# Pairing the experts of a mixture layer to the last one, and moving a run-time branch behind the last expert's products

## The chip, the cores and the metric

The kernel runs on one core of a Trainium2 chip. Its engines are named as in the profile: PE is TensorE (matrix products) and PEld its weight loads, DVE is VectorE, ACT is ScalarE, POOL is GpSimd, and SP is SyncE, which here issues nearly all DMAs. The metric is the device time of one execution in microseconds (us), taken as the median of several runs. A profiled execution has a span (first to last instruction) and its own time, which is slightly longer.

## The reference

Two layers, each a mixer (three kinds of attention) followed by a hierarchical mixture of experts over 256 tokens with 1024 channels. The change is in the mixture:

```python
def hier_moe(h, w_gr, b_gr, w_er, b_er, w1, w3, w2):
    ...   # top-1 group of 4, top-2 of its 8 experts: 512 assignments to 32 experts
    def expert_ffn(args):
        xb, e = args
        return (jax.nn.silu(xb @ w1[e]) * (xb @ w3[e])) @ w2[e]
    ...   # rows gathered in blocks of one expert, results weighted and added back per token
x = x + gt2 * hier_moe(h, ...)
```

w1 and w3 are 1024 x 384 and w2 is 384 x 1024 for each of the 32 experts, all float32.

## The kernel before

The order of the work on each engine is written out by hand: every engine executes its instructions in the order in which the Python code emits them, and waits on semaphores where data or a buffer is missing. A matrix product is emitted through the helper `mm` (line 102), so nearly all products carry that line and are told apart by the tiles that they write: `A` (first products of an expert), `O` (second products), `y` (the sums per token), `ga` (the gather), `uT` (transposes), `PTe` (one-hot transposes).

`moe(l)` gives each expert a block of 64 slots. One-hot matrices (`onehot`, line 1557) gather the tokens of four experts at a time: `gather_piece(q, i)` does 8 products into a bank `ga`, which ACT scales out into `xT` (line 1582); four pieces make one group of four experts. Then a loop runs over the experts e = 0 to 31. Its parts are:

- `ffn1(e)`: 16 products with w1 and w3 into `A` (recorded as two groups of 16 instructions, one for each of the two weight pieces of 1536 KB), on even e also `places` (line 1594), then silu on ACT (line 1632) and gate and product on DVE (line 1633) into `u`. Two experts of a pair share one `u`, in its two halves of 64 partitions, where `paired(e)` holds.
- `tr_pair(e)` (lines 1646 and 1648): three transposes of a whole pair's `u` and one ACT copy to `uT`; or `tr(e)` (lines 1658 and 1661): the same for one expert.
- `ffn2(e)`: 6 products (12 instructions) with w2, the third weight piece, into `O`, then two DVE products with the layer's gate (line 1693). After the odd expert of a pair, ACT and DVE split the result into two parts (lines 1699 and 1700).
- `combine(p, js)`: products that add the parts of pair p into the four `y` banks, one half of the channels for each j.

The loop is staggered up to e = 23: it emits ffn1(e), a half of an older combine, tr_pair on odd e, two gather pieces on odd e up to 27, and then ffn2(e-1), so that the second products of an expert stand behind the first ones of the next. From e = 24 (`ATONCE`) on each expert is done at once: ffn1(e), combine, gather, tr(e), ffn2(e). The last pair is combined behind the loop, straight from float32.

`overflow` (from line 1789) handles experts with more than 64 tokens. Every engine loads a count from SBUF into a register (line 1794) and branches over a loop (line 1798) that is entered only where the count is above zero; with these inputs it isn't entered. Behind the branch each engine sets semaphores, since waits behind it count on what the loop would have signalled. Before the change it stands ahead of ffn1(30).

The weights come as one stream of DMAs in a fixed order (`pump`, line 85): 94 pieces of 1536 KB for the experts' loop of a layer and 6 smaller ones that are loaded ahead. A piece is issued when fewer than `ring` pieces are held (6, and 8 from e = 26), so when PE is through with an older one. Behind layer 0's experts the stream goes on with layer 1's mixer: a piece of its input projection, then pieces of the modulation (`ada`).

Behind the loop of layer 0 the next mixer's first steps are emitted (`next(self.mixing)`), then combine(15); in layer 1 combine(15) is followed by the copies and the DMAs of the output.

Of the kernel before, what the change touches and what calls it, by code (L numbers as in the profile page):

```python
# [17 lines left out]
NE, SLOTS = 32, 64  # L18
# [19 lines left out]
class Kern:  # L38
# [1373 lines left out]
    def moe(self, l):  # L1412
# [15 lines left out]
        y = [[self.bank('y') for _ in range(2)] for _ in range(2)]  # L1428
# [4 lines left out]
        xhi, xlo = ([self.alloc('w', [128, 1024], F32R, 'xp') for _ in range(2)] for _ in range(2))  # L1433
# [37 lines left out]
        Mf, G, R = (RT[:, i * 64:i * 64 + 64].rearrange("p (t n) -> p t n", t=2) for i in range(3))  # L1471
# [21 lines left out]
        gt = self.gate_halves(l)  # L1493
# [34 lines left out]
        def blocks():  # L1528

            cnt, nb, cum, tt = (RT[:, 192 + 32 * i:224 + 32 * i] for i in range(4))  # L1530
            V.tensor_scalar(nb, cnt, float(SLOTS), None, op0=ALU.is_gt)
            for k in (2, 3):
                V.tensor_scalar(tt, cnt, float(SLOTS * k), None, op0=ALU.is_gt)
                V.tensor_add(nb, nb, tt)
            cur, other = cum, tt
            V.tensor_copy(cur, nb)
            for s in (1, 2, 4, 8, 16):
                V.tensor_copy(other[:, :s], cur[:, :s])
                V.tensor_add(other[:, s:32], cur[:, s:32], cur[:, :32 - s])
                cur, other = other, cur  # L1540
            nov = self.cp.tile([128, 4], I32, name=f"nov_{l}", tag='nov')
            V.tensor_copy(nov[:, 0:1], cur[:, 31:32])
            start = RT[:, 320:352]
            V.tensor_sub(start, cur, nb)
            return nov, nb, start
        a2, s2 = ab[:, 0:8], ab[:, 8:16]
# [13 lines left out]
        def onehot_b(q):  # L1560
            V.tensor_copy(PO[q][1], PO[q][0])

        def gather_piece(q, i):

            P, _ = PO[q]
            if i == 0:
                for h in range(2):
                    XT[q, h] = self.alloc('w', [128, 8, 128], F32, 'xT')
            ps = self.bank('ga')
            for k in range(2):  # L1570
                kt = 2 * i + k
                n = 0
                for t in range(2):
                    for part in (xhi, xlo):
                        self.mm(ps[:, k * 256:k * 256 + 256], part[t][:, kt * 128:kt * 128 + 128],
                                P[:, t].rearrange("p e s -> p (e s)"), n == 0, n == 3)
                        n += 1
            for k in range(2):
                kt = 2 * i + k
                for h in range(2):  # L1580
                    dst, src = XT[q, h][:, kt], ps[:, k * 256 + h * 128:k * 256 + h * 128 + 128]
                    nc.scalar.activation(dst, src, AF.Identity, scale=a2[:, kt:kt + 1], bias=s2[:, kt:kt + 1])  # L1582
            self.free(ps)
# [52 lines left out]
            E[e] = u  # L1636

        def paired(e):
            return e < ATONCE

        def tr_pair(e):

            u = E[e]
            p = self.bank('uT')
            for f in range(3):
                nc.tensor.transpose(p[:, f * 128:f * 128 + 128], u[:, f * 128:f * 128 + 128], self.ident)
            uT = self.alloc('s', [128, 3, 128], F32, 'uT')
            nc.scalar.activation(uT, p[:, :384].rearrange("p (f s) -> p f s", f=3), AF.Copy)
            self.free(p, u)
            E[e - 1], E[e] = uT[:, :, 0:64], uT[:, :, 64:128]  # L1650
            UT[e] = uT

        def tr(e):
            u = E[e]
            b = 64 * (e % 2)
            p = self.bank('uT')
            for f in range(3):
                nc.tensor.transpose(p[:, f * 64:f * 64 + 64], u[b:b + 64, f * 128:f * 128 + 128],  # L1658
                                    self.ident[b:b + 64, b:b + 64])
            uT = self.alloc('s', [128, 3, 64], F32, 'uT')  # L1660
            nc.scalar.activation(uT, p[:, :192].rearrange("p (f s) -> p f s", f=3), AF.Copy)  # L1661
            self.free(p, u)
            E[e] = UT[e] = uT
# [3 lines left out]
        def ffn2(e):  # L1667
            uT = E[e]
            key = ('e', l, e, 2)
            if key in self.beside(l):  # L1670
                w = [self.pieces[key + (f,)] for f in range(3)]
            else:
                u = self.take(key)
                w = [u[:, 1024 * f:1024 * f + 1024] for f in range(3)]
            n = 256 if e == NE - 1 else 512
            o = {c: self.bank('O') for c in range(0, 512, n)}
            for c in range(0, 512, n):
                for f in range(3):
                    for h in range(2):
                        self.mm(o[c][64 * h:64 * h + 64, :n], uT[:, f], w[f][:, 512 * h + c:512 * h + c + n], f == 0, f == 2)  # L1680
            if key in self.beside(l):
                self.free(*w)
            else:
                self.done(key)
            if e in UT:
                self.free(UT.pop(e))
            if e % 2 == 0:
                O[e // 2] = self.alloc('w', [128, 1024], F32, 'O')
            b = 64 * (e % 2)
            for c in range(0, 512, n):  # L1690
                for h in range(2):
                    p = slice(64 * h, 64 * h + 64)
                    V.tensor_mul(O[e // 2][b:b + 64, 512 * h + c:512 * h + c + n], o[c][p, :n], gt[p, c:c + n])  # L1693
            self.free(*o.values())
            if e % 2 and e < NE - 1:

                whole = O[e // 2]
                hi, lo = O[e // 2] = [self.alloc('w', [128, 1024], F32R, 'Op') for _ in range(2)]
                nc.scalar.activation(hi, whole, AF.Copy)  # L1699
                V.tensor_sub(lo, whole, hi)  # L1700
                self.free(whole)

        def combine(p, js=(0, 1)):
            last = p == 15
            parts = [O[p]] if last else O[p]
            for j in js:
                n = 256 if last else 512
                for c in range(0, 512, n):
                    for t in range(2):
                        to = PT[p][:, t * 128:t * 128 + 128]  # L1710
                        for part in parts:
                            self.mm(y[t][j][:, c:c + n], to.bitcast(F32) if last else to, part[:, 512 * j + c:512 * j + c + n],
                                    False, last and c + n == 512)
            if js[-1]:
                self.free(*parts)
                if p % 2:
                    self.free(PTQ[p // 2])


        ATONCE = 24  # L1720

        def rest_of_first():
            gather_piece(0, 2)
            gather_piece(0, 3)
            onehot(1)
            onehot_b(1)

        onehot(0)
        gather_piece(0, 0)
        gather_piece(0, 1)  # L1730
        G3 = gates_and_blocks()
        onehot_b(0)
        nov, nb, start = blocks()
        for e in range(NE):
            if e == NE - 6:
                self.ring = 8
            if e == ATONCE:
                ffn2(e - 1)
            if e == NE - 2:
                self.overflow(l, xhi, xlo, R, G, nb, start, nov, gt, a2, s2, y)  # L1740
            if e:
                ffn1(e)
            else:
                ffn1(0, rest_of_first)
            if 4 <= e < ATONCE + 2:
                combine(e // 2 - 2, (e % 2,))
            if e < ATONCE and e % 2:
                tr_pair(e)
            if e // 4 < 7 and (e % 2 if e > 3 else e > 1):
                for i in range(2):  # L1750
                    gather_piece(e // 4 + 1, (e % 4 - 1 if e > 3 else 2 * e - 4) + i)
                if e % 4 == 3 and e // 4 < 6:
                    onehot(e // 4 + 2)
                    onehot_b(e // 4 + 2)
            if e >= ATONCE:
                combine(e // 2 - 1, (e % 2,))
                tr(e)
                ffn2(e)
                continue
            if e:  # L1760
                ffn2(e - 1)
        self.free(*xhi, *xlo)
        if self.mixing:
            nc.scalar.preload_act_table_set(EXP_LN)
# [211 lines left out]
```

## Time and profile before

| | |
|---|---|
| median of 3 runs | 1390.2 us (1389.4 to 1391.21) |
| profiled execution, its own time | 1390.37 us |
| span of that execution | 1388.6 us |
| PE busy | 1329.2 us (96%) |
| PEld, DVE, ACT, POOL busy | 63%, 48%, 39%, 10% of the span |
| DMA | 437.95 MB, mean 315 GB/s |
| mean granted TensorE clock | 0.989 |

The experts' loop of layer 0 runs from about 369 to 715 us of the span, that of layer 1 from about 1038 to 1384 us. The granted clock is a share of 2.4 GHz; the other level is 1.2 GHz. A busy PE includes products that run at the slower level.

### The profile page before, as it was taken

How to read it: one execution, taken by the hardware profiler on the slowest of the kernel's cores; microseconds unless marked ns; L12 is line 12 of the kernel's file. 1: busy time of each engine (PE TensorE's matmuls, PEld its weight loads, DVE VectorE, ACT ScalarE, POOL GpSimd, SP SyncE). 2: the span in 40 equal slices, each digit the busy share in tenths (PEclk: the TensorE clock that was granted, in tenths of full speed). 3: DMA queues.
4: the chain of work that ended last, by engine and by line, in shares of the span. 5: the costliest groups of instructions: out<-in, count | busy, mean ns of one | idle time of the engine just before them, and what ended most of it. 6: DMA issues, size and time to landing. Idle time of an engine off the chain costs nothing. (4 is left out here: it accounts for less than half of the span.)

```text
span 1388.6 us, 19465 instructions
## 1 busy us (share of the span) xinstructions
PE 1329.2 (96%) x7666; PEld 869.3 (63%) x7666; DVE 668.2 (48%) x1417; ACT 538.4 (39%) x1140; POOL 135.2 (10%) x138
## 2 busy tenths in 40 slices
PE   5999999999899999999899999999999999999997
PEld 3788787887544444444358897888764444444443
DVE  5587564676623223332256775556762233323222
ACT  4554554574322222221155565447532222222211
POOL 0002064300100000000000202641010000000000
PEclk9999999999999999999999999999989999999999
DMA  9965457369589999999993626525858999999993
GB/s 373 374 246 222 184 204 289 129 246 360 222 345 425 425 425 424 425 426 425 420 421 151 227 91 232 191 94 202 358 214 318 404 425 425 425 424 427 424 424 147
DMA packets 45215, 437.95 MB, mean 315 GB/s; under 512 B 5080, under 2 KB 5608, under 8 KB 11328
## 3 DMA queue, kind: packets, MB, share of 16 engines
q1 hardware_dynamic: 44832, 435.78, 77.2%
q8 instruction: 62, 1.02, 0.3%
q0 software_dynamic: 288, 0.89, 0.2%
q14 instruction: 33, 0.27, 0.1%
HBM read 435.59 MB, written 1.05 MB: 314 GB/s over the span
## 5 line engine op out<-in xcount | busy, mean ns | idle before, releaser
L102 PE MATMUL in<-h,hH 128*128 128x384 f32 (+1 forms) x576 | 206.1, 358 | 3.7 <-ACT hH L1345 2.5
L1693 DVE TENSOR_TENSOR O<-O,gth 64x512 f32<-64x512 f32 (+1 forms) x132 | 88.8, 673 | 243.2 <-PE O L102 242.2
L102 PE MATMUL in<-h,hL 128*128 128x384 f32 (+1 forms) x576 | 195.3, 339 | 0.1
L102 PE MATMUL in<-l,hH 128*128 128x384 f32 (+1 forms) x576 | 194.5, 338 | 0.0
L1632 ACT ACTIVATE u<-A 64x384 f32<-64x384 f32 x64 | 31.1, 487 | 300.9 <-PE A L102 300.9
L102 PEld LDWEIGHTS in<-h,hH 128*128 128x128 f32 x576 | 109.0, 189 | 29.3 <-issue 17.1
L102 PEld LDWEIGHTS in<-h,hL 128*128 128x128 f32 x576 | 108.8, 189 | 1.4 <-DVE hL L1346 1.4
L102 PEld LDWEIGHTS in<-l,hH 128*128 128x128 f32 x576 | 109.2, 190 | 0.5
L1582 ACT ACTIVATE xT<-ga,modab 128x128 f32<-128x128 f32 x256 | 93.0, 468 | 20.6 <-PE ga L102 20.6
L1699 ACT ACTIVATE Op<-O 128x1024 fp32r<-128x1024 f32 x30 | 31.7, 1057 | 138.6 <-DVE O L1693 138.6
L1633 DVE SCALAR_TENSOR_TENSOR u<-A,m,u 64x384 f32<-64x384 f32 x64 | 39.4, 616 | 89.5 <-ACT u L1632 86.1
L102 PE MATMUL ga<-Poh,xp 128*128 128x256 f32 x512 | 71.4, 294 | 0.0
L102 PE MATMUL y<-Op,PTp 128*128 128x512 f32 x240 | 70.1, 415 | 0.0
L102 PEld LDWEIGHTS ga<-Poh,xp 128*128 128x128 f32 x512 | 65.8, 198 | 5.4 <-issue 4.0
L1602 DVE CAST PTp<-PTe 128x256 fp32r<-128x256 bf16 x32 | 13.6, 425 | 115.3 <-PE PTe L102 115.3
L803 POOL TENSOR_TENSOR rot<-TB,rope 128x256 f32<-128x256 f32 x8 | 11.7, 1487 | 488.6 <-ACT UC L873 429.3
L947 ACT ACTIVATE P<-P,m 128x256 f32<-128x256 f32 (+1 forms) x48 | 27.6, 576 | 79.2 <-DVE m L1005 37.1
L102 PEld LDWEIGHTS y<-Op,PTp 128*128 128x128 f32 x240 | 40.6, 188 | 21.0 <-issue 15.5
L1700 DVE TENSOR_TENSOR Op<-O,Op 128x1024 fp32r<-128x1024 f32 x30 | 36.8, 1225 | 33.8 <-ACT Op L1699 29.2
L1033 POOL TENSOR_SCALAR bias<-dist 128x128 f32<-128x128 f32 (+1 forms) x48 | 36.5, 761 | 5.2 <-PE oT L102 1.3
L1030 POOL TENSOR_SCALAR qz<-UC,gq 128x384 f32<-128x384 f32 x16 | 22.2, 1387 | 142.9 <-PE oT L102 72.7
L955 DVE TENSOR_SCALAR P<-P,m 128x256 f32<-128x256 f32 (+1 forms) x80 | 29.9, 407 | 1.8
(848 smaller groups left out, 2451.5 us busy)
## 6 DMA issues: line engine op xcount, KB each, us to landing
piece<-in_w_e SPq DMA_DIRECT2D x12, 512.0 KB, 6.8
w('ada', 0, 0, 0)_4_90<-in_w_ada SPq DMA_DIRECT2D x1, 1536.0 KB, 9.6
w('ada', 0, 0, 1)_5_92<-in_w_ada SPq DMA_DIRECT2D x1, 1536.0 KB
w('in', 0, 0)_9_104<-in_w_in SPq DMA_DIRECT2D x2, 768.0 KB, 16.5
w('in', 0, 1)_10_108<-in_w_in SPq DMA_DIRECT2D x2, 768.0 KB, 16.3
w('in', 0, 2)_11_110<-in_w_in SPq DMA_DIRECT2D x2, 768.0 KB, 12.2
w('ada', 0, 0, 3)_18_196<-in_w_ada SPq DMA_DIRECT2D x1, 1536.0 KB
w('ada', 0, 0, 4)_35_252<-in_w_ada SPq DMA_DIRECT2D x1, 1536.0 KB
```

The costliest lines, as they stand in the source:

```text
L102: self.nc.tensor.matmul(out, lhsT, rhs, start=start, stop=stop)
L947: nc.scalar.activation(dst, src, AF.Exp, bias=mx_neg[:, i:i + 1], scale=1.0, accum_out=sm[:, i:i + 1])
L955: nc.vector.tensor_scalar(dst, dst, r[:, i:i + 1], None, op0=ALU.mult)
L1030: nc.gpsimd.tensor_scalar(qz, M['qd'][:, pr::2, t * 128:t * 128 + 128], self.gq[:, l, 1 + hh:2 + hh], None, op0=ALU.mult)
L1033: nc.gpsimd.tensor_scalar(bias[:, lo:hi], self.dist[:, t, 256 + lo:256 + hi], -DIL_SLOPE[g][h], None, op0=ALU.mult)
L1582: nc.scalar.activation(dst, src, AF.Identity, scale=a2[:, kt:kt + 1], bias=s2[:, kt:kt + 1])
L1602: V.tensor_copy(PT[p], pv)
L1632: nc.scalar.activation(u[b:b + 64], A[c:c + 64, :384], AF.Silu)
L1633: V.scalar_tensor_tensor(u[b:b + 64], A[b:b + 64, :384], GC[e // 2][b:b + 64, e % 2:e % 2 + 1], u[b:b + 64], op0=ALU.mult, op1=ALU.mult)
L1693: V.tensor_mul(O[e // 2][b:b + 64, 512 * h + c:512 * h + c + n], o[c][p, :n], gt[p, c:c + n])
L1699: nc.scalar.activation(hi, whole, AF.Copy)
L1700: V.tensor_sub(lo, whole, hi)
```

## The change

The loop is staggered to the end: each expert's second products stand behind the next one's first products, ffn2(31) stands behind the loop, and behind it combine(14), the overflow branch, and combine(15). All experts but the first two are paired. The first two are transposed one by one, expert e-1 behind ffn1(e). In the turn of e = 3 the transposes of the pair are put between the products of the gather's first piece and that piece's ACT copies. The number of products is the same; the transposes of e = 24 to 31 become 4 pairs of them, those of e = 0 and 1 two single ones.

```diff
-        def gather_piece(q, i):
+        def gather_piece(q, i, between=None):
...
+            if between:
+                between()
             for k in range(2):
                 kt = 2 * i + k
                 for h in range(2):
...
         def paired(e):
-            return e < ATONCE
+            return e > 1
...
-        ATONCE = 24
...
         for e in range(NE):
             if e == NE - 6:
                 self.ring = 8
-            if e == ATONCE:
-                ffn2(e - 1)
-            if e == NE - 2:
-                self.overflow(l, xhi, xlo, R, G, nb, start, nov, gt, a2, s2, y)
             if e:
                 ffn1(e)
             else:
                 ffn1(0, rest_of_first)
-            if 4 <= e < ATONCE + 2:
+            if e >= 4:
                 combine(e // 2 - 2, (e % 2,))
-            if e < ATONCE and e % 2:
+            if 0 < e < 3:
+                tr(e - 1)
+            elif e % 2 and e > 3:
                 tr_pair(e)
             if e // 4 < 7 and (e % 2 if e > 3 else e > 1):
                 for i in range(2):
-                    gather_piece(e // 4 + 1, (e % 4 - 1 if e > 3 else 2 * e - 4) + i)
+                    gather_piece(e // 4 + 1, (e % 4 - 1 if e > 3 else 2 * e - 4) + i,
+                                 (lambda: tr_pair(3)) if e == 3 and i == 0 else None)
                 if e % 4 == 3 and e // 4 < 6:
                     onehot(e // 4 + 2)
                     onehot_b(e // 4 + 2)
-            if e >= ATONCE:
-                combine(e // 2 - 1, (e % 2,))
-                tr(e)
-                ffn2(e)
-                continue
             if e:
                 ffn2(e - 1)
+        ffn2(NE - 1)
+        combine(14)
+        self.overflow(l, xhi, xlo, R, G, nb, start, nov, gt, a2, s2, y)
         self.free(*xhi, *xlo)
```

## Rows read from the trace of the kernel before

**Rows 1.** Windows: length, each engine's busy time (instructions), clock, DMA share, GB/s.

```profile
1287.26:1359.99 72.73, 65.46 (x373) 30.52 (x369) 19.94 (x32) 14.72 (x32) 0.00 (x0) 1.00 1.01 422
```

**Rows 2.** Timeline of PE, staggered experts of layer 1: start, length, instruction, [idle before].

```profile
1225.01 2.75 PE L102 MATMUL A<-'e', 1, 18, 0)_2041_9981,xT 128*64 128x384 f32 x16
...
1234.18 2.75 PE L102 MATMUL A<-e', 1, 19, 0)_2053_10057,xT 128*64 128x384 f32 x16
...
1240.76 0.55 PE L1646 MATMUL uT<-pk,u 128*128 128x128 f32 x3
...
1245.77 2.75 PE L102 MATMUL A<-e', 1, 20, 0)_2064_10109,xT 128*64 128x384 f32 x16
```

**Rows 3.** Timeline of PE, layer 1 from expert 24 to the branch.

```profile
1287.26 2.74 PE L102 MATMUL O<-e', 1, 23, 2)_2105_10344,uT 128*64 128x512 f32 x12
1289.84 2.75 PE L102 MATMUL A<-e', 1, 24, 0)_2109_10361,xT 128*64 128x384 f32 x16
...
1295.28 2.08 PE L102 MATMUL y<-Op,PTp 128*128 128x512 f32 x8
...
1359.99 0.54 PE L102 MATMUL A<-e', 1, 30, 0)_2183_10776,xT 128*64 128x384 f32 x2 [2.63 <-ACTq L1798]
```

**Rows 4.** Timeline, first experts: one row of layer 0, then layer 1.

```profile
384.31 2.79 PE L102 MATMUL O<-piece,uT 128*64 128x512 f32 x12 [0.58 <-ACT uT L1648]
...
1051.40 0.48 ACT L1632 ACTIVATE u<-A 64x384 f32<-64x384 f32 x1 [5.07 <-PE A L102]
...
1052.60 0.55 PE L1646 MATMUL uT<-pk,u 128*128 128x128 f32 x3 [1.24 <-DVE u L1633]
...
1053.73 4.49 PE L102 MATMUL O<-piece,uT 128*64 128x512 f32 x12 [0.58 <-ACT uT L1648]
...
1074.77 0.55 PE L1646 MATMUL uT<-pk,u 128*128 128x128 f32 x3 [1.24 <-DVE u L1633]
```

**Rows 5.** Instructions of line 1661: count, ns min/median/max, first and last start.

```profile
L1661 ACT ACTIVATE uT<-uT x16: 331/332/369, 626.6 to 1377.5; 128x192 f32<-128x192 f32 x16
```

**Rows 6.** Timeline of SP's DMA issues, three weight pieces.

```profile
665.82 0.33 SPq L85 DMA_DIRECT2D 'e', 0, 31, 0)_1093_5416<-in_w_e  x1
...
689.19 0.33 SPq L85 DMA_DIRECT2D ada', 1, 1, 0)_1110_5498<-in_w_ada  x1
...
1336.95 0.33 SPq L85 DMA_DIRECT2D e', 1, 31, 0)_2195_10851<-in_w_e  x1
```

**Rows 7.** DMA issues of the same pieces; the last number is us from issue to landing.

```profile
'e', 0, 31, 0)_1093_5416<-in_w_e SPq DMA_DIRECT2D x1, 1536.0 KB, 22.4
ada', 1, 1, 0)_1110_5498<-in_w_ada SPq DMA_DIRECT2D x1, 1536.0 KB, 14.0
...
e', 1, 31, 0)_2195_10851<-in_w_e SPq DMA_DIRECT2D x1, 1536.0 KB, 21.4
```

**Rows 8.** Timeline of PE, ends of both layers' experts.

```profile
688.87 4.50 PE L102 MATMUL A<-'e', 0, 30, 0)_1081_5341,xT 128*64 128x384 f32 x16 [2.63 <-DMA 'e', 0, 31, 2)_1104_5464<-in_w_e]
...
703.57 2.75 PE L102 MATMUL A<-'e', 0, 31, 1)_1101_5447,xT 128*64 128x384 f32 x16
...
714.83 1.48 PE L102 MATMUL ada<-ada', 1, 1, 0)_1110_5498,cond 128*32 128x512 f32 x10
...
1373.00 2.75 PE L102 MATMUL A<-e', 1, 31, 1)_2203_10882,xT 128*64 128x384 f32 x16
...
1377.00 0.40 PE L1658 MATMUL uT<-pk,u 64*128 64x64 f32 x3
...
1380.62 3.72 PE L102 MATMUL y<-O,PTp 128*128 128x256 f32 x16
```

**Rows 9.** Sequencer instructions of the branch, line 1798, on PE in layer 1.

```profile
L1798 PEldq COMPARE_BRANCH x1: 323/323/323, 1355.0 to 1355.0; - x1
...
L1798 PEldq EVENT_SEMAPHORE  x1: 51/51/51, 1357.4 to 1357.4; - x1
```

**Rows 10.** Windows as in rows 1, early in layer 1's experts.

```profile
1080.00:1083.00 3.00, 3.00 (x20) 1.29 (x18) 1.38 (x2) 0.00 (x0) 0.00 (x0) 1.00 0.70 217
```

## The prediction

> **What bounds the kernel now.** I read the page first (PE busy 96%, the DMA engines full for long stretches), then windows over the experts' loops, then the timelines of PE and of SP's DMA issues side by side. In the loops both look full: over the late experts of layer 1 PE is busy 65.46 of 72.73 us while the DMA share is 1.01 at 422 GB/s [rows 1]. The question is which of the two waits for the other. A weight piece of 1536 KB (1.573 MB) takes 3.73 us at 422 GB/s, an expert's three pieces 11.2 us. In the staggered part PE takes 9.17 us from A of an even expert to A of the odd one (1225.01 to 1234.18) and 11.59 us on to the next (1234.18 to 1245.77), with no product waiting for a DMA [rows 2]: 10.4 us per expert. So PE is faster than the stream and eats up the lead that the ring gave it, without having used it up. From expert 24 on PE loses time that is not products: it stands 7.3 us in the stretch of rows 1, of which 2.63 us are the wait at the overflow branch ahead of expert 30, where the releaser is ACT's semaphore at line 1798 [rows 3]. The rest are waits for u and uT, one expert at a time. There the order on PE sets the time, not the weights.
>
> **The first experts.** Before, A(1) is followed by the pair's transposes, which need u(1): PE stands 1.24 us, then 0.58 us for the ACT copy, and O(0) starts at 1053.73 [rows 4]. After, u(0) is long there. Its ACT copy stands behind silu(1), which ends at 1051.88 [rows 4]; with the single transposes' copy of 0.33 us [rows 5] and some 0.1 us of handing over O(0) starts at 1052.3: 1.4 us gained. In turn 2 the second single transpose costs PE some 0.3 us. In turn 3 the wait of 1.24 us ahead of the pair's transposes [rows 4] is filled by the gather piece's eight products (about 1.0 us, half of what 16 take); 1.0 us gained. The later ACT copies of that piece are used only by expert 4. Sum: 1.4 - 0.3 + 1.0 = 2.1 us in each layer; from below 0.7 (only the wait for the copy and a little more), from above 3.0. In layer 1 O(0) took 4.49 us where layer 0's same group, behind the same waits, took 2.79 [rows 4]: products at the 1.2 GHz level after PE had stood. With 0.6 us of standing left instead of 1.82 I count the 1.7 us as gained; the ends are 0 and 1.7.
>
> **The late experts, up to the last first product.** O(23) no longer stands ahead of A(24), so A(24) starts at 1287.26, not 1289.84 [rows 3]. With the steps of rows 2, A(25) starts at 1296.43, A(26) at 1308.02, A(27) at 1317.19, A(28) at 1328.78, A(29) at 1337.95. The turn of 29 has no gather to cover the ACT copy: 6.58 us to the transposes (1234.18 to 1240.76), 1.13 us from them to O (1052.60 to 1053.73), 2.6 us for O: 10.3 us. So A(30) could start at 1348.25 and A(31) at 1357.42, where it is 1370.42 now (1373.00 less the 2.58 us of one weight piece's products). Now the weights answer: piece (31, 0) is issued at 1336.95 [rows 6] and lands 21.4 us later [rows 7], at 1358.35, 12.1 us ahead of its use now, but 0.9 us behind what PE could do after. The last expert becomes bound by the stream: A(31)'s second half starts at 1358.35 + 2.58 = 1360.9 instead of 1373.00 [rows 8], a gain of 12.1 us. The other late pieces land 3.73 us apart and bind at most by as much: (30, 1), two pieces earlier, lands at 1350.9 and would be wanted at 1350.83.
> In layer 0 the same piece is issued at 665.82 and lands 22.4 us later, at 688.22 [rows 6, 7]; the second half starts at 690.8 instead of 703.57 [rows 8], a gain of 12.8 us, of which 1.7 is A(30)'s slow clock behind the branch (4.50 us for 2.75) [rows 8], since the idle 2.63 us ahead of it is gone. Both gains hold wherever the early 2.1 us put the stream, if the stream moves with them (below).
>
> **The end.** Before, from A(31)'s second half to the last group of y takes 7.62 us (1373.00 to 1380.62), the transposes standing at 4.00 (1377.00) [rows 8]. After: transposes at 4.00, O(30) at 4.00 + 1.13 = 5.13, O(31) at 7.73, combine(14) at 10.35 with the 2.08 us that eight such products take [rows 3], last y group at 12.43. That is 4.8 us longer in each layer: one second product (2.6) and one whole combine (2.1) now stand behind the last weights. DVE's products with the gate for expert 31 end about 0.9 us before that group, so they don't hold it.
>
> **The branch behind the products.** Queued behind it are on PE the last y group, on ACT and DVE layer 1's first splits or the output copies, on SP only pieces for which no one waits yet. ACT and DVE reach it early or with that cover of 0.9 us. On PE the branch stands at 1355.0 and its semaphore at 1357.4, just when O(29)'s products are through [rows 9]: the jump took place under running products, as it will under combine(14)'s 2.08 us. What is left is letting the products run out, about 0.4 us. The ends are 0 and 2.63 us, the whole idle time of now [rows 3]; I take the low value because no engine behind it is late any more.
> What the trace can't show is the jump by itself, as it is covered by 2.0 us of products. The Trainium skill, "Runtime: NRT & Kernel Launch", section "Instruction fetch mechanics", says that a taken branch whose target is not in the fetched stretch has to wait for a DMA of the target's page. It speaks against a branch on the path; the rows bear it out only as far as 2.0 us may be hidden, and the first rival below is what it would do here.
>
> **Layer 0's gain on its way.** Layer 1's modulation piece (ada 1, 1, 0) is issued at 689.19 [rows 6] and lands 14.0 us later at 703.2 [rows 7]; it is used at 714.83 [rows 8]. The stream moves 2.1 us, PE about 9.7, so 7.6 of the 11.6 us are used up. The next piece, 3.7 us later in the stream and used half a us later, keeps about 0.8 us. All of the gain passes, with little to spare.
> For the stream to move with PE it must run empty after the early turns: in layer 1 its share is still 0.70 between 1080 and 1083 [rows 10], so the next issue, not the queue, dates it, and that issue follows PE.
>
> **Sum.** Layer 0: 2.1 + 12.8 - 4.8 - 0.4 = 9.7. Layer 1: 2.1 + 1.7 + 12.1 - 4.8 - 0.4 = 10.7. Together 20.4 us. The profiled execution took 1390.37 us, 0.2 above the median, so 1370.0 us.
>
> **Rivals.**
> *The branch shows* (0.14). PE drains behind combine(14) and then waits for another engine's semaphore or for the jump's target, as it waits for ACT now. Against it: the engines reach the branch earlier than PE. Price: 2.63 instead of 0.4 in each layer, 4.5 us: 1374.5.
> *The stream stands still* (0.12). If the queue is full before the early gain is made, the landings keep their dates and the early 2.1 + 2.1 + 1.7 = 5.9 us are lost, as the last expert waits for its landing: 1375.9. Against it stands rows 10; for it, that layer 0's pieces land 1.0 us later than layer 1's [rows 7], so its queue is fuller.
> *The weights decide already* (0.04), the case on the other side. If pieces landed just before their use, nothing ahead of the last expert could gain and only the longer end would count: 2 x (4.8 + 0.4) = 10.4 us, 1400.8. It decides where the lead at (31, 0) is below 5.2 us; it is 12.1 now. It needs the stream to deliver late once PE crowds it.
> *No change* (0.03): a blend of these with the gains just eaten up, near 1390.
>
> **How the numbers follow.** The forecast case has 0.65, and its own range is 1366.5 to 1373.5: 1.7 us more or less for each spell at the slow level, since the small waits left could also lower the clock, and the branch anywhere from 0 to 1. The remaining 0.02 is for more gain than that. A range of 1366.5 to 1377.5 takes in the first two rivals with half a spell; below 0.2 is left out. This kernel's measurement tells about 0.2% (2.8 us) from no change: faster 0.93, same 0.03, slower 0.04.
>
> **What would show it.** In the profile after: no idle of over 1 us ahead of A(30); A(31) waiting for a DMA, not for ACT; 12.4 us from its second half to the last y group; that group behind combine(14) with under 1 us of idle; O(0) at full clock in both layers. Wrong would be an idle of 2 us or more at the branch, PE waiting for landings from expert 25 on, or layer 1's mixer starting with a wait for a modulation piece.

## The result, and the profile after

The changed kernel takes 1369.0 us in the median of four runs (1367.6 to 1369.5), the kernel before 1390.0 us beside it (1389.4 to 1391.2): a ratio of 0.9846, with a 95% interval of 0.9829 to 0.9863. Faster by 20.9 us; 1370.0 had been predicted, with a saving of 20.4.

The page of the profiled execution after (its own time 1369.49 us): span, then busy time of each engine, its share and its instructions.

```profile
span 1367.6 us, 19428 instructions
...
PE 1324.1 (97%) x7648; PEld 868.0 (63%) x7648; DVE 668.4 (49%) x1417; ACT 537.7 (39%) x1134; POOL 135.4 (10%) x138
```

PE's busy time fell by only 5.1 us (1329.2 before), the span by 21.0. So most of what went is idle time. Of the 5.1 us, 3.4 are two groups that ran in part at the slow clock before, O(0) of layer 1 [rows 4] and A(30) of layer 0 [rows 8], and run at full speed now. Among the late experts of layer 1, from A(24) to the start of O(28), PE is now busy 57.43 of 58.42 us, with the DMA engines as full as in [rows 1]. Windows, columns as there:

```profile
1273.11:1331.53 58.42, 57.43 (x332) 26.82 (x328) 17.12 (x27) 13.38 (x28) 0.00 (x0) 1.00 1.01 425
```

The timeline of PE in layer 1: the first experts, the pair's transposes of turn 3, and the end.

```profile
1041.83 2.80 PE L102 MATMUL O<-piece,uT 128*64 128x512 f32 x12 [0.61 <-ACT uT L1663]
...
1060.28 1.22 PE L102 MATMUL ga<-Poh,xp 128*128 128x256 f32 x8
1061.59 0.55 PE L1648 MATMUL uT<-pk,u 128*128 128x128 f32 x3
1061.89 1.19 PE L102 MATMUL ga<-Poh,xp 128*128 128x256 f32 x8
...
1334.15 2.75 PE L102 MATMUL A<-e', 1, 30, 0)_2175_10776,xT 128*64 128x384 f32 x16
...
1340.93 2.79 PE L102 MATMUL O<-e', 1, 29, 2)_2169_10729,uT 128*64 128x512 f32 x12
1344.39 2.80 PE L102 MATMUL A<-e', 1, 31, 0)_2185_10825,xT 128*64 128x384 f32 x16 [0.66 <-SPq L1794]
1346.99 2.78 PE L102 MATMUL A<-e', 1, 31, 1)_2189_10842,xT 128*64 128x384 f32 x16
...
1351.00 0.55 PE L1648 MATMUL uT<-pk,u 128*128 128x128 f32 x3
1352.13 2.80 PE L102 MATMUL O<-e', 1, 30, 2)_2179_10800,uT 128*64 128x512 f32 x12 [0.58 <-ACT uT L1650]
1354.75 2.76 PE L102 MATMUL O<-e', 1, 31, 2)_2190_10855,uT 128*64 128x256 f32 x24
1357.44 2.11 PE L102 MATMUL y<-Op,PTp 128*128 128x512 f32 x8
1359.71 3.69 PE L102 MATMUL y<-O,PTp 128*128 128x256 f32 x16
```

Four things are to be seen. O(0) starts behind a wait of 0.61 us at full speed, where [rows 4] had waits of 1.24 and 0.58 us and 4.49 us of products. The pair's transposes of turn 3 stand between two halves of a gather piece, with no wait. A(30) starts without the 2.63 us of [rows 3], and A(31) waits 0.66 us. Its releaser is named as SP's queue at the branch, but the issue and the landing show what it is. In SP's timeline:

```profile
1317.40 0.33 SPq L85 DMA_DIRECT2D e', 1, 31, 0)_2185_10825<-in_w_e  x1
```

and in the list of DMA issues, where a time to the landing is given for layer 0's twin:

```profile
'e', 0, 31, 0)_1092_5411<-in_w_e SPq DMA_DIRECT2D x1, 1536.0 KB, 26.9
```

1317.40 + 26.9 = 1344.3, just ahead of A(31) at 1344.39. In layer 0 the trace names the DMA itself, and in the kernel without the branch (below) it does so in layer 1 too. Layer 0, with its end, which answers to [rows 8]:

```profile
685.48 2.80 PE L102 MATMUL A<-'e', 0, 31, 0)_1092_5411,xT 128*64 128x384 f32 x16 [0.72 <-DMA 'e', 0, 31, 0)_1092_5411<-in_w_e]
688.08 2.78 PE L102 MATMUL A<-'e', 0, 31, 1)_1096_5428,xT 128*64 128x384 f32 x16
...
704.44 1.48 PE L102 MATMUL ada<-ada', 1, 1, 0)_1104_5478,cond 128*32 128x512 f32 x10
```

The sequencer's instructions of the branch (now lines 1790 and 1794), as in [rows 9]: for each engine's queue the count, the durations and the first and last start.

```profile
L1790 PEldq TENSOR_LOAD <-nov x2: 316/402/488, 697.2 to 1356.1; - x2
...
L1794 PEldq COMPARE_BRANCH  x2: 236/289/342, 697.8 to 1356.5; - x2
...
L1794 DVEq COMPARE_BRANCH  x2: 56/64/72, 699.3 to 1358.0; - x2
L1794 DVEq EVENT_SEMAPHORE  x2: 21/21/21, 699.7 to 1358.6; - x2
L1794 PEldq EVENT_SEMAPHORE  x2: 51/51/51, 700.7 to 1359.6; - x2
```

PE loads the count and branches at 1356.1 to 1356.8, under O(31)'s and combine(14)'s products, and sets its semaphore at 1359.6, when these are through; the last group of y starts at 1359.71. DVE branches later than PE, at 1358.0, but its semaphore at 1358.6 is still 1.0 us ahead of PE's.

Laid beside the steps of the prediction, all in us, profiled execution against profiled execution:

| step | predicted | layer 0 | layer 1 |
|---|---|---|---|
| early: A(4), from the layer's A(0) | 2.1; 3.8 in layer 1 with the clock | 1.99 | 3.67 |
| A(31)'s second half, from A(0), in all | 14.9; 15.9 | 15.49 | 15.54 |
| from there to the last group of y | 5.2 longer | 5.13 longer | 5.10 longer |
| net, to the end of that group | 9.7; 10.7 | 10.4 | 10.4 |

Layer 0's gain passes whole: layer 1's A(0) moves from 1038.16 to 1027.69. The 20.9 us between the end of PE's work before (1380.62 + 3.72) and after (1363.40) are the 20.9 between the medians.

### The profile page after: what moved, and what is told of

Same layout as the page of the kernel before. It is cut to its first block, busy times and chain, and to the rows that moved or that the text cites. A ratio compares the mean times of both kernels' runs of the same rounds, so it can differ in the third digit from the quotient of the medians.

```text
span 1367.6 us, 19428 instructions
## 1 busy us (share of the span) xinstructions
PE 1324.1 (97%) x7648; PEld 868.0 (63%) x7648; DVE 668.4 (49%) x1417; ACT 537.7 (39%) x1134; POOL 135.4 (10%) x138
```

## The experiments

Twelve kernels, all run beside the kernel before. Ratios are to it. They were measured in three series, in which the kernel before took 1389.1, 1389.5 and 1390.0 us; microseconds saved are counted from the one of the same series.

### The branch alone

The kernel before, with the call of `overflow` taken from the loop and put ahead of combine(15).

```diff
-            if e == NE - 2:
-                self.overflow(...)
...
         self.free(*xhi, *xlo)
+        self.overflow(...)
```

> The kernel before with one edit: the branch goes from ahead of expert 30 to behind the loop, ahead of combine(15); experts 24 to 31 stay one at a time. My theory: the idle 2.63 us ahead of A(30) goes in both layers, and in layer 0 the 1.7 us of slow clock behind it; the last experts still have about 9 us of lead on their weights, so nothing takes it back: about 7 us less, less some 0.4 for the drain at the end, 1383.4 (1382.5 to 1385.5). Rival (the branch costs as much wherever it stands): 1389 to 1391.

1383.1 us (1381.2 to 1385.3), ratio 0.9961 (0.9948 to 0.9973): 6.0 us saved, of the 21. The idle time ahead of A(30) is gone in both layers. But in layer 0 the last group of y started, stopped and went on. Timeline of PE there, then of DVE, and the semaphores that both set behind the branch (first start in layer 0, last start in layer 1):

```profile
706.86 1.10 PE L102 MATMUL y<-O,PTp 128*128 128x256 f32 x4 [0.16 <-PEq L1797]
709.15 2.86 PE L102 MATMUL y<-O,PTp 128*128 128x256 f32 x12 [1.19 <-DVE l L598]
```

```profile
706.74 0.88 DVE L1693 TENSOR_TENSOR O<-O,gth 64x256 f32<-64x256 f32 x2 [0.42 <-PE O L102]
707.68 0.06 DVE L1792 MEMSET it<- 128x1 f32 x1
707.96 1.83 DVE L598 TENSOR_TENSOR l<-w('in', 1, 0)_1105_5476,h 128x768 fp32r<-128x768 f32 x2 [0.21 <-DVEq L1797]
```

```profile
L1797 PEldq EVENT_SEMAPHORE  x2: 51/51/51, 706.8 to 1373.3; - x2
...
L1797 DVEq EVENT_SEMAPHORE  x2: 21/21/21, 707.8 to 1374.3; - x2
```

Here no combine(14) stands between O(31) and that group, and PE is past the branch 1.0 us ahead of DVE. The trace names as the releaser DVE's first split for the next mixer (line 598), the first work that DVE does past the branch. But the group doesn't read that split, and DVE's products with the gate for expert 31, which it does read, had ended at 707.62. In layer 1 DVE is as late, no split stands there, and the group ran through. The kernels that fill the waits (below) have the same lateness and the same splits in layer 0, and their group runs through as well. So neither DVE's lateness nor the splits alone explain the stop of 1.19 us. Its cause stays open; a wait of PE's own behind its jump is not excluded.

The run also shows that the slow O(0) of [rows 4] does not belong to a layer. The order up to there is that of the kernel before, and the waits ahead of O(0) are the same 1.24 and 0.58 us in both layers, but now layer 0 has the slow group (4.49 us) and layer 1 the fast one (2.79). Timeline of PE, then windows of this kernel; the last column but two is the granted clock:

```profile
382.51 4.49 PE L102 MATMUL O<-piece,uT 128*64 128x512 f32 x12 [0.58 <-ACT uT L1648]
...
1050.75 2.79 PE L102 MATMUL O<-piece,uT 128*64 128x512 f32 x12 [0.58 <-ACT uT L1648]
```

```profile
382.51:385.50 2.99, 2.99 (x10) 1.07 (x12) 0.00 (x0) 0.00 (x0) 0.00 (x0) 0.64 1.01 427
1050.75:1053.50 2.75, 2.75 (x14) 1.04 (x16) 0.00 (x0) 0.00 (x0) 0.00 (x0) 1.00 1.01 425
```

Behind the same waits the clock falls in some executions to the 1.2 GHz level for a part of the group, in others not.

### The branch back, in the staggered order

The changed kernel with `overflow` ahead of ffn1(30) again.

```diff
+            if e == NE - 2:
+                self.overflow(...)
             if e:
                 ffn1(e)
...
         combine(14)
-        self.overflow(...)
```

> The changed kernel with the branch put back ahead of A(30), the staggering kept. My theory: the old 2.63 us were not the jump but ACT, which reached the branch only behind its split of O(29); in the staggered order ACT has nothing of the kind there, so PE stands some 0.2 us, and the last expert waits 0.7 us for its landing anyway. So the time is that of the changed kernel, 1369.0 within 0.8 us. Rival (the place of the branch is what gained): 2.63 us of idle in each layer, of which the landing hides 0.8, and more with a slow clock: 1372.5 to 1376.

1370.3 us (1367.8 to 1371.0), ratio 0.9869 (0.9847 to 0.9890). That is 0.5 us above the expected range and 2.2 below the rival's. The expectation missed the idle time: not 0.2 but 1.60 us ahead of A(30), in both layers. Timeline of PE, then of DVE:

```profile
1336.47 2.80 PE L102 MATMUL A<-e', 1, 30, 0)_2175_10776,xT 128*64 128x384 f32 x16 [1.60 <-DVEq L1795]
```

```profile
1334.92 1.39 DVE L1695 TENSOR_TENSOR O<-O,gth 64x512 f32<-64x512 f32 x2 [4.08 <-PE O L102]
1336.25 0.06 DVE L1790 MEMSET it<- 128x1 f32 x1
```

ACT, the late engine of [rows 3], set its semaphore early (1332.3). DVE took its place: it comes to the branch only behind its two products with O(28), which end at 1336.31. Only 0.4 to 0.5 us of the 1.60 reach the last group of y (counted from A(0), against the profile of the changed kernel), since A(31) then finds its weights landed and doesn't wait. The place of the branch is worth about half a microsecond a layer once the order is staggered, and 3 us in the old order; the two gains overlap. The half microsecond is read from the profiles; in the times it is not clear of the noise.

### The first experts alone

The kernel before with the single transposes of experts 0 and 1 and the pair's transposes between the gather's products.

```diff
-                tr_pair(e)
...
+            if 0 < e < 3:
+                tr(e - 1)
+            elif e < ATONCE and e % 2 and e > 3:
+                tr_pair(e)
...
+                                 (lambda: tr_pair(3)) if e == 3 and i == 0 else None)
```

> The kernel before with the part of the change on experts 0 to 3 alone (two single transposes, the pair of 3 between gather piece and its copies). My theory: 2.0 us less in layer 0, 3.7 in layer 1 (1.7 of it clock), all of it passed on, since PE and not the stream sets the time there: 1384.3 (1383.5 to 1386.5). Rival (the stream sets the time, so an early gain is lost): 1389 to 1390.5.

1382.9 us (1381.6 to 1384.5), ratio 0.9958 (0.9946 to 0.9970): 6.2 us saved, a little more than expected (1383.5 was the low end). A(4) starts 37.94 us behind A(0) in both layers, as in the changed kernel (39.93 and 41.62 before), and all of it arrives at the end. In layer 0 another 1.7 us arrive with it: A(30) runs at full speed here, behind the same 2.63 us at the branch behind which it took 4.50 us before [rows 8]. Timeline of PE:

```profile
687.30 2.80 PE L102 MATMUL A<-'e', 0, 30, 0)_1084_5348,xT 128*64 128x384 f32 x16 [2.63 <-ACTq L1803]
...
1352.95 2.80 PE L102 MATMUL A<-e', 1, 30, 0)_2189_10790,xT 128*64 128x384 f32 x16 [2.63 <-ACTq L1803]
```

So the slow group is no more tied to its place here than at O(0).

### The late experts alone

The changed kernel with the old first turns: all experts paired, transposes on odd e only.

```diff
-            return e > 1
+            return True
...
-            if 0 < e < 3:
-                tr(e - 1)
-            elif e % 2 and e > 3:
+            if e % 2:
                 tr_pair(e)
```

> The changed kernel with the first four experts as before. The last expert is bound by its landing, so this tells whether the stream moves with PE's early gain. My theory: it does, and the time grows by 2.0 + 3.7 to about 1374.7 (1373 to 1376). Rival (the stream stands still, the landings keep their dates): 1369 to 1370.5.

1372.7 us (1372.4 to 1375.0), ratio 0.9894 (0.9874 to 0.9915): 16.4 us saved. With the 6.2 of the first experts alone that is 22.6, for 20.9 to 21.7 with both. It tells the forecast from the rival in which the stream stands still: then the early part would bring nothing, and this kernel would have taken 1369 to 1370.5. A(31) starts 319.08 and 318.72 us behind A(0), 2.3 and 2.0 later than in the changed kernel, and still waits for its weights; timeline of PE:

```profile
1347.83 2.48 PE L102 MATMUL A<-e', 1, 31, 0)_2179_10811,xT 128*64 128x384 f32 x14 [0.74 <-SPq L1791]
```

PE and the stream move by the same 2 us. Both of this kernel's layers had a fast O(0), so 4 us of the early part are what is missing here; measured were 3.6 from median to median, or 4.5 with each counted from the kernel before beside it. The 1374.7 expected had counted on a slow O(0), which is why the time came out just below the range (1373).

### A second branch

The changed kernel with the call of `overflow` twice in a row; the second has its own counter and no products to cover it.

```diff
         self.overflow(...)
+        self.overflow(..., 'b')
```

> The changed kernel with the overflow branch emitted twice, one right behind the other; neither loop is entered. The second jump has no products to hide under, so its whole price shows. My theory: load of the register, compare and jump are 0.3 to 0.5 + 0.3 + at most 0.5 us as the queues of ACT and SP show, 1.2 us in each layer: 1371.4 (1370.3 to 1372.5). Rival (a taken branch has to fetch code; the 2.0 us that products covered were needed): 2 us or more in each layer, 1373 or above.

1372.3 us (1371.6 to 1374.1), ratio 0.9879 (0.9864 to 0.9894). The timeline of PE shows the idle time behind both branches:

```profile
1361.06 3.69 PE L102 MATMUL y<-O,PTp 128*128 128x256 f32 x16 [1.22 <-PEq L1795]
```

It is 1.23 us in layer 0. From A(31)'s second half to the last group of y are 13.80 and 13.79 us, for 12.74 and 12.72 with one branch, so the second branch, which has no products to cover it, costs 1.1 us. The Trainium skill, "Runtime: NRT & Kernel Launch", section "Instruction fetch mechanics", the page that spoke against a branch on the path, says that a taken branch out of the fetched stretch waits for a DMA of its target. If there is such a wait here, it is inside these 1.1 us, with the load of the count (0.3 us on PE) and the branch itself (0.24 to 0.46 us over the four of this kernel). No run separates them.

### No branch

The changed kernel without the call of `overflow`.

> The changed kernel without the overflow branch (left out is the work for experts with over 64 tokens, of which these inputs have none). If the branch under combine(14) costs what the trace shows, 0.16 us of idle per layer and some emission around it, the time is 1368.6 (1367.8 to 1369.2). Rival, that the branch still costs something like its old wait of 2.6 us per layer in a place that shows as other work: 1363.8. In between, that the DVE products of expert 31 and not the branch hold the last y group: no change, 1369.0, with the same 0.2 us of idle, put down to DVE.

1367.6 us (1366.8 to 1368.6), 0.7 less than the changed kernel beside it in the same series (1368.3, below). The two ranges overlap, so the time excludes the rival of 1363.8 but does not show the 0.7 by itself; the trace does. Timeline of PE:

```profile
1343.14 2.80 PE L102 MATMUL A<-e', 1, 31, 0)_2173_10669,xT 128*64 128x384 f32 x16 [0.70 <-DMA e', 1, 31, 0)_2173_10669<-in_w_e]
1345.75 2.78 PE L102 MATMUL A<-e', 1, 31, 1)_2177_10686,xT 128*64 128x384 f32 x16
...
1358.15 3.61 PE L102 MATMUL y<-O,PTp 128*128 128x256 f32 x16
```

From A(31)'s second half to the last group are 12.40 us, in both layers, for 12.74 and 12.72 with the branch. So the branch under combine(14) costs 0.33 us a layer, about what it takes to let PE's products run out.

### More of the ring

The changed kernel with `ring` = 8 from the first expert on, instead of from e = 26.

```diff
-            if e == NE - 6:
+            if e == 0:
                 self.ring = 8
```

> The changed kernel with 8 pieces held from the first expert on instead of from expert 26. The stream runs empty now and then over the first experts, so two pieces more in flight bring its landings forward. My theory: the last expert waits 0.7 us for its landing in each layer and only that can go: 1367.5 (1367 to 1368.2). Rival (the stream is full anyhow, its rate decides): 1369.0. Second rival (the whole of it is stream-bound): several us less.

1369.6 us (1369.1 to 1370.6), ratio 0.9855 (0.9840 to 0.9870): no change, where 1367.5 had been expected. Piece (8, 0) of layer 1 is issued 49.89 us behind A(0), 49.91 in the changed kernel. The description of the kernel says that a piece is issued when fewer than `ring` pieces are held; on the chip that is not what dates it. SP works through its own queue and issues a piece as soon as one of the ten buffers is free: (31, 0) at 1317.40, when A(28)'s first products (1314.60 + 2.58) let go of theirs, with the nine others still held or on their way. `ring` only places the instruction in the order of the code.

### One weight piece less

Expert 20's second products take the piece that its first ones still hold, and its third piece isn't loaded.

```diff
-            order += [('e', l, e, u) for e in range(NE) for u in range(3) if ('e', l, e, u) not in self.beside(l)]
+            order += [... and (e, u) != (20, 2)]
...
-                if kt % 4 == 3:
+                if kt % 4 == 3 and key[2:] != (20, 1):
                     self.done(key)
...
-            key = ('e', l, e, 2)
+            key = ('e', l, e, 1 if e == 20 else 2)
```

> The changed kernel with one weight piece less per layer: expert 20's second products use the piece of its own second w1/w3 part, so it computes with other weights and moves 3.1 MB less; the number of products is the same. The last landing comes 3.7 us earlier. My theory is that in the changed kernel PE is only 0.7 us ahead of the last landing and bound by its own order everywhere before: the wait at A(31) goes, 0.7 us per layer, 1367.6 us (1366.8 to 1368.4). Rival, that the stream sets PE's pace through the whole loop: 3.7 us per layer, 1361.6.

1367.0 us (1364.9 to 1368.8), 1.3 less than the changed kernel beside it, where a kernel bound by its stream all the way would have gained 7.5 (one piece a layer). The 1.3 alone is within the spread of the runs; the place shows in the timeline of PE:

```profile
1340.97 2.79 PE L102 MATMUL O<-e', 1, 29, 2)_2167_10725,uT 128*64 128x512 f32 x12
1343.60 2.75 PE L102 MATMUL A<-e', 1, 31, 0)_2183_10821,xT 128*64 128x384 f32 x16
1346.18 2.75 PE L102 MATMUL A<-e', 1, 31, 1)_2187_10838,xT 128*64 128x384 f32 x16
```

A(31) follows O(29) without a wait, and its second half starts 318.20 us behind A(0) in both layers, 1.1 earlier than in the changed profile. Up to A(30) nothing moves (306.46 for 306.47). So the stream is the bound of the last expert alone, by 1.1 us: 0.7 of wait at A(31) and the rest in small waits inside A(30) and A(31). Right behind it stands PE's own order.

### The last combines as filling

A try for a faster version: combine(13)'s second half behind O(29), where A(31) waits; combine(14)'s halves ahead of and behind the last transposes, where PE waits for u and uT; the branch right behind O(31).

```diff
-            if e >= 4:
+            if e == NE - 1:
+                combine(14, (0,))
+            elif e >= 4:
                 combine(e // 2 - 2, (e % 2,))
...
+            if e == NE - 1:
+                combine(14, (1,))
             if e:
                 ffn2(e - 1)
+            if e == NE - 2:
+                combine(13, (1,))
         ffn2(NE - 1)
-        combine(14)
```

> A version meant to be better: combine(13)'s second half stands behind O(29), where PE waits for the last landing; combine(14)'s first half covers the wait for u(31), its second half the ACT copy ahead of O(30); the branch follows O(31). My theory: of 12.7 us from A(31)'s second half to the last y group, one combine half (1.0) and the waits (0.6 us of ACT copy, 0.2 at the branch) go, and 0.4 us of waiting for DVE comes: about 1.6 us in each layer, 1365.8 (1365 to 1367.5). Rival (DVE's products with the gate for expert 31 become the wait): no change, 1368 to 1369.

1367.5 us (1365.4 to 1367.9), ratio 0.9837 (0.9824 to 0.9851), at the upper end of what had been expected. The same with the ring at 8:

> The same with 8 pieces held from the first expert on. My theory: the last landing no longer holds A(31), and 0.7 us more go in each layer: 1364.3 (1363.5 to 1366). Rival: the same as with 6 pieces, 1365.8.

1367.3 us (1366.8 to 1367.7), ratio 0.9838 (0.9825 to 0.9852): again the ring changes nothing, and the expected 1364.3 was missed by 3 us. Then once more, side by side with the changed kernel as it is:

> The changed kernel as it is, side by side with the next one: 1369.0 us (1368.0 to 1370.0), A(31) waiting about 0.7 us for its weights in both layers. If the earlier difference of 1.5 us to the kernel with moved combines was chance, the two come out within 0.5 us of each other.

1368.3 us (1367.7 to 1369.0), ratio 0.9846 (0.9832 to 0.9860).

> The kernel with combine(13) and combine(14) put into the waits, again. Its last y group stood 1.2 and 1.4 us earlier after A(0) in the two layers, so 2.6 us less than the changed kernel beside it: 1366.4 (1365.5 to 1367.5). Rival: the gain is chance, 1369.0.

1367.6 us (1366.1 to 1368.5), ratio 0.9842 (0.9828 to 0.9856), for 1366.4 expected. Its timeline of PE, the last group of layer 0 and the end of layer 1:

```profile
698.10 3.69 PE L102 MATMUL y<-O,PTp 128*128 128x256 f32 x16 [0.16 <-PEq L1799]
...
1342.09 1.20 PE L102 MATMUL y<-Op,PTp 128*128 128x512 f32 x4
1343.21 2.80 PE L102 MATMUL A<-e', 1, 31, 0)_2185_10825,xT 128*64 128x384 f32 x16
...
1353.88 2.76 PE L102 MATMUL O<-e', 1, 31, 2)_2190_10855,uT 128*64 128x256 f32 x24
1356.80 3.69 PE L102 MATMUL y<-O,PTp 128*128 128x256 f32 x16 [0.16 <-PEq L1799]
```

The waits at A(31) and O(30) are filled, and the last group of y comes 1.5 and 1.4 us sooner behind A(0) than in the profile beside it. In the times it is less: over both series the medians are 1367.6 (10 runs) and 1368.5 (9 runs), with ranges that overlap. That is under the 0.2% that this kernel's measurement can tell, so the version is at best a microsecond faster, and that is not shown.

The end shows something else. The branch stands right behind O(31) here, without combine(14), and DVE's semaphore comes 1.0 us behind PE's (1357.7 and 1356.7 in layer 1). The last group of y starts 0.16 us behind O(31) all the same and runs through, in both layers of all three profiled executions of this order.

## Why the prediction was right

**What bounds the kernel.** The reading that the order on PE and not the stream sets the time, with 12 us of lead at the last piece, held: the third rival (1400.8) would have needed A(31) to wait for a DMA before. What the full DMA engines hid was that the queue was long, not late. The steps of rows 2 carried to the end give the order after to within a tenth: from A(24) to A(28) 41.5 us predicted, 41.49 measured.

**The first experts.** 2.1 predicted, 1.99 measured in layer 0 (O(0) 1.44 us sooner, for 1.4; 0.42 lost in the turn of 2, for 0.3; 0.97 gained in the turn of 3, for 1.0), and 2.0 in the kernel with this part alone (39.93 to 37.94), in which no O(0) was slow. The clock's 1.7 us, counted as a gain of layer 1, did come out between the two profiled executions, but by chance: in the three profiled kernels with the old first turns (before, the branch alone, the late part alone) two of six O(0) groups were slow, in the eleven with the new ones none of 22. So the gain is an average of some 0.6 us a layer by that count (an estimate, 1.7 x 2/6), and the 1.7 belonged to one execution. That the clock falls less often because PE stands for 0.61 us instead of 1.82 fits the counts; no run varied that wait by itself.

**The last expert.** Predicted was that the landing of (31, 0) would bind by 0.9 us; A(31) waits 0.7, and takes 1.1 us less with a shorter stream. In layer 1 the late part brought 15.54 - 3.67 = 11.9 for 12.1. In layer 0 it brought 15.49 - 1.99 = 13.5 for 12.8: that term was too small by 0.7. The landing there moved 2.87 us (688.22 to 658.45 + 26.9 = 685.35), not 2.1. Behind A(0) that is 319.48 before and 316.61 after, and so it is 316.6 in layer 1 (1344.3 - 1027.69). I had let the stream move with PE's 2.1 us alone; part of the 1.0 us by which layer 0's piece took longer [rows 7] went too. Where it came from no run shows. That it was the early part that pulled the stream along is shown by the kernel without it: both PE and landings are 2 us later there. The 1.7 us of slow clock at A(30) in layer 0's 12.8 are of the same kind as those at O(0): of four groups behind the 2.63 us at the branch, in the profiles of the kernel before and of the first experts alone, one was slow.

**The end.** 5.2 us longer predicted, 5.1 measured: transposes at 4.01, O(30) at 5.14, O(31) at 7.76, combine(14) at 10.45, the last group at 12.72 in layer 1, without the branch at 12.40 for 12.43.

**The branch.** 0.4 us a layer predicted, 0.33 measured by taking it away. But the reason as I put it, that the engines reach the branch earlier than PE and none is late any more, is not what the runs show. In the old place DVE is late in the staggered order too: 1.60 us of idle, where ACT's lateness had cost 2.63. In the new place DVE still branches behind PE (1358.0 and 1356.5). What makes it cheap is that PE has products queued while it jumps. That need not be combine(14): behind O(31) alone, with DVE later than PE, the wait is 0.16 us in both layers of the kernels that fill the waits and in layer 1 of the kernel with the branch alone. Where nothing covers the jump, it costs 1.1 us. The one stop that doesn't fit, 1.19 us in layer 0 of the kernel with the branch alone, stays unexplained. The rival in which the branch shows was priced at 2.63 by the old wait; that wait was ACT's lateness, and a bare branch costs less than half of it.

**Sizes in sum.** 9.7 + 10.7 predicted, 10.4 + 10.4 measured: layer 0's landing gave 0.7 more, layer 1's late part 0.2 less. The sum came closer than its terms deserve: one slow spell in each layer (O(0) in layer 1, A(30) in layer 0; 3.4 us together) fell into the profiled execution that I worked from. By the granted clock other executions of the kernel before had fewer of them: in the first series of experiments the fastest took 1385.7 us at a mean granted clock of 0.993, the slowest 1391.2 us at 0.989.

## What to carry to other kernels

Where two resources look full, ask for the lead of the last transfer that the path needs: 12 us of lead made this stream harmless until the order on PE caught up with it, and after that the next microsecond has to come from both. Put a branch that all engines must pass where the engine on the path still has two microseconds of queued work to run, and look at every engine's lateness there, not only at the one that the trace names, for the next one is close behind. A gain that only one execution shows at one place (here a slow clock spell) is looked up in the other layer and in other executions before it enters the sum.

## What was not expected of the hardware

The clock fell behind the same two waits of 1.24 and 0.58 us in two of six cases, and in no fixed layer (granted 0.64 over 3 us, 1.7 us lost), and behind 2.63 us in one of four. A branch taken over an unused loop costs PE 1.1 us with nothing to run under it, 0.33 us under 2.1 us of products. DMA pieces were issued by the freeing of one of ten buffers, whatever the order of emission allowed, and waited in a queue of some seven pieces (an estimate: 26.9 us from issue to landing, 3.73 us a piece).
